# First adaLN modulation in fp32 column groups, and the sums of the later modulations moved to ScalarE and POOL

## The chip, the cores and the metric

One core of a Trainium2 chip runs the whole program. The metric is device time in microseconds, the median of several executions. Besides, one execution was recorded by the profiler.

## What is computed

A diffusion backbone of two layers works on 256 latent tokens and 256 context tokens of 1024 channels. Each layer begins with a modulation: the conditioning vector goes through SiLU and a matrix of 1024 x 6144, which gives six vectors of 1024 channels (shift, scale and gate for each of two sub-layers), for the latent and for the context stream:

```python
mod_lat = (silu_c @ w_mod[l] + b_mod[l])[:, None, :]
mod_ctx = silu_cc @ w_mod[l] + b_mod[l]
sh1, sc1, gt1, sh2, sc2, gt2 = jnp.split(mod_lat, 6, axis=-1)
h = rms_norm(x, g_pre_mix[l]) * (1.0 + sc1) + sh1
y, yc = token_mixer(h, hc, w_in[l], ...)
x = x + gt1 * rms_norm(y, g_post_mix[l])
h = rms_norm(x, g_pre_mlp[l]) * (1.0 + sc2) + sh2
x = x + gt2 * rms_norm(squared_relu_mlp(h, w_mlp_in[l], w_mlp_out[l]), g_post_mlp[l])
```

The context stream goes through the same with its own modulation; in the second layer only the latent stream is written. The token mixer has three branches (retention, neighbourhood attention, grouped-query attention) and large projections; the MLP widens to 4096. Everything is fp32.

## The kernel before

Large products are made of three fp32r matmuls: each operand is split in a rounded part (a cast on ScalarE, tiles `wh`, `pwh`) and the rest (a subtraction on VectorE, `wl`, `pwl`), and hi x hi, hi x lo and lo x hi are summed (`mm3`, line 185). Weights come in blocks of 128 x 1024 (512 KB) on SP's queue, loaded three ahead and split two ahead of the step that uses them (`ahead`, line 1411).

**The prologue** (line 243) does the first modulation (shift and scale of the first sub-layer, layer 0), the normalisation of the 512 tokens and the first product (queries and keys of the retention branch, `pr`). It goes in four quarters `kp` of 256 channels. For each, four blocks of `w_mod` and one of `w_in` are loaded. All five are split. `mod` (line 287) multiplies the conditioning vectors, stationary in `msr` (two columns of the rounded part, two of the rest, zeros up to 128), with 32 matmuls of 256 columns into `modps`; `row` (298) copies four rows out on ScalarE; `fin` (306) turns them into columns with four small matmuls (`pm`, eight records in the trace) that add the bias row; VectorE makes shift and scale; `pre_tr` transposes the normalised tokens (`ph`); `pre_h` applies scale and shift on ScalarE and splits the result on VectorE (`hT`); `gemm` (318) makes the quarter's 24 matmuls. The order of all this is written out by hand in `PLAN` (line 56): c splits up to a block, a is `mod`, t `pre_tr`, r `row`, f `fin`, h `pre_h`, g `gemm`. While `Ordered.on` is set, each engine keeps the program's order. The normalisation is a chain of small VectorE operations for each of four token tiles (`pre_xn`).

**The later modulations** (`mod_dve`, line 403) aren't on TensorE. For each of ten vectors, eight blocks `mr` of `w_mod` are loaded on POOL's queue, into two buffers; for each block and stream VectorE does one operation, acc = block x scalar + acc (`stt`, in `step`, line 459), the first one with the bias row `brow` in place of acc. Two streams: six of the vectors, one stream: four; 128 operations in all. Then the partitions are summed by TensorE: with ones (gates, `pg`) or, for shift and scale, with a stationary of 32 columns in column groups of 32 output partitions (`pmr`, line 432). The steps of three vectors are woven into the end of layer 0's mixer (line 1344), those of six more into its MLP, the last into layer 1's MLP.

The scheduler that comes with the language fixes each engine's order of instructions; `tc.issue_after(ins)` puts the instructions of a block behind `ins` in the queue of `ins`'s engine.

Of the kernel before, what the change touches and what calls it, by code (L numbers as in the profile page):

```python
# [9 lines left out]
F32 = mybir.dt.float32  # L10
# [20 lines left out]
MLB = 2  # L31
NT = 8
NB2 = 5
C1 = 0
WR = 3
WH = 3
WLD = 3
# [11 lines left out]
XLATE = True  # L49
END = ((0, 0), (1, 0))  # L50
ORD = ((0, 4, 5), (0, 4, 8))
RW = 2
PLD = 4
PAD, PAD2, WP = 432, 272, 1152
FILL = (((0, 9), (9, 21), (21, 33)), ((0, 9), (7, 22), (22, 39)))
PLAN = ["c4 t0 a0 c5 r0 f0 h0 c9 g0 c13",
        "a1 t1 r1 c14 f1 h1 c18",
        "a2 r2 c19 g1 t2 f2 h2",
        "a3 t3 r3 c20 f3 h3 g2"]


class Ordered:
# [20 lines left out]
def kernel(  # L83
# [47 lines left out]
    def S(name, dt=F32R):  # L131
        return sp.tile([128, 2, 512], dt, tag="s", name=name)
# [31 lines left out]
    def tt(o, a, b, op):  # L164
        return v_.tensor_tensor(out=o, in0=a, in1=b, op=op)
# [36 lines left out]
    selr = const.tile([4, 512], F32R, tag="selr", name="selr")  # L202
    cc = const.tile([128, 8, 2], F32, tag="cc", name="cc")
    cs = const.tile([128, 8, 2], F32, tag="cs", name="cs")
    ones = const.tile([128, 128], F32R, tag="ones", name="ones")
    oneh = const.tile([128, 32], F32, tag="oneh", name="oneh")
    onesf = const.tile([128, 128], F32, tag="onesf", name="onesf")
# [33 lines left out]


    def prologue():
        pr = []
        M = {}
        raw, rdy = {}, {}
        md = lambda kp: [wspec(w_mod[0], 512 * hf, 4, v * D + 256 * kp, 256) for v in range(2) for hf in range(2)]
        gm = lambda kp: [wspec(w_in[0], 256 * kp, 2, RQ, 512)]
        wts = md(0) + gm(0) + md(1) + gm(1) + md(2) + gm(2) + md(3) + gm(3)
        mi = (0, 5, 10, 15)  # L250
        gi = (4, 9, 14, 19)

        def load(n):
            while len(raw) < min(n, len(wts)):
                i = len(raw)
                ap, k, *_ = wts[i]
                t = S("pr", F32) if i % RW else wrp.tile([128, 2, 512], F32, tag="wr", name="pr")
                raw[i] = t
                st["hold_sp"] = nc.sync.dma_start(
                    out=t.rearrange("p a b -> p (a b)").rearrange("p (k n) -> p k n", k=k), in_=ap)  # L260

        def cut(n):
            while len(rdy) < min(n, len(wts)):
                i = len(rdy)
                load(i + PLD)
                t, k = raw[i], wts[i][1]
                hi = wtile(whp, "wh", "pwh").rearrange("p (a b) -> p a b", a=2) if i % 3 == 0 else S("pwh")
                lo = wtile(wlp, "wl", "pwl").rearrange("p (a b) -> p a b", a=2) if i % 3 == 0 else S("pwl")
                st["hold_act"] = s_.copy(hi, t)
                st["hold"] = tt(lo, t, f(hi), ALU.subtract)  # L270
                rdy[i] = [u.rearrange("p a b -> p (a b)").rearrange("p (k n) -> p k n", k=k) for u in (hi, lo)]

        def init():
            msr = S("msr")
            zero = T("zero")
            v_.memset(zero, 0.0)
            v_.tensor_copy(msr[:, 0, :], zero)
            v_.tensor_copy(msr[:, 1, :], zero)
            msr = msr.rearrange("p a b -> p (a b)").rearrange("p (k m) -> p k m", k=8)
            v_.tensor_copy(msr[:, :, 0:2], cs)  # L280
            tt(msr[:, :, 2:4], cs, f(msr[:, :, 0:2]), ALU.subtract)
            M["msr"] = msr
            for n_ in ("sh1", "sc1"):
                st[0, n_] = smp.tile([128, 8, 2], F32, tag=n_, name=n_, bufs=2)
            pr.extend(mmt(f"pr{i}") for i in range(4))

        def mod(kp):
            ps = att("modps")
            for i in range(4):
                v, hf = i // 2, i % 2  # L290
                w = rdy[mi[kp] + i]
                for k in range(4):
                    for p in range(2):
                        t_.matmul(ps[:, 256 * v:256 * v + 256], M["msr"][:, 4 * hf + k, :], w[p][:, k, :],
                                  start=(hf == 0 and k == 0 and p == 0), stop=(hf == 1 and k == 3 and p == 1))
            M["ps", kp] = ps

        def row(kp):
            s_.copy(st["r5", kp][0:4, :], M["ps", kp][0:4, :])

        def bias(kp):
            r5 = st["r5", kp] = T("r5")
            nc.gpsimd.dma_start(out=r5[4:5, :].rearrange("o (v n) -> o v n", v=2),
                                in_=b_mod[0:1, 0:2 * D].rearrange("o (v n) -> o v n", v=2)[:, :, 256 * kp:256 * kp + 256])

        def fin(kp):
            r5 = st.pop(("r5", kp))
            pt = att("pm")
            for j in range(4):
                t_.matmul(pt[:, 2 * j:2 * j + 2], r5[0:5, 128 * j:128 * j + 128], sel[0:5, 18:20],  # L310
                          start=True, stop=True)
            p3 = pt[:, 0:8].rearrange("p (j e) -> p j e", e=2)
            hs = slice(2 * kp, 2 * kp + 2)
            v_.tensor_copy(st[0, "sh1"][:, hs, :], p3[:, 0:2, :])
            for s in range(2):
                stt(st[0, "sc1"][:, hs, s], p3[:, 2:4, s], 1.0, gp[:, 0, hs], ALU.add, ALU.mult)

        def gemm(kp):
            w_ = rdy[gi[kp]]
            for k in range(2):  # L320
                for i in range(4):
                    kc = 2 * kp + k
                    w = slice(128 * i, 128 * i + 128)
                    mm3(pr[i], (w_[0][:, k, w], w_[1][:, k, w]), hpair(kc, 512), kc == 0, kc == 7)

        def go(ws):
            Ordered.on = True
            load_x(4)
            load(PLD)
            for kp in range(2):  # L330
                bias(kp)
            init()
            sq = [pre_sq(0)]
            pre_xn(0, sq[0])
            sq.append(pre_sq(1))
            cut(C1)
            pre_xn(1, sq[1])
            for kp, plan in enumerate(PLAN):
                for c in plan.replace("_", " ").split():
                    o, n = c[0], int(c[1:])  # L340
                    if o == "c":
                        cut(n)
                    elif o == "a":
                        mod(n)
                    elif o == "r":
                        row(n)
                    elif o == "t":
                        ph = [pre_tr(n, s) for s in range(2)]
                    elif o == "f":
                        fin(n)  # L350
                        if n < 2:
                            bias(n + 2)
                    elif o == "h":
                        h32 = [T("h32") for _ in range(2)]
                        for j in range(2):
                            for s in range(2):
                                pre_h(0, 0, n, s, ph[s], (j,), h32[s])
                    elif o == "g":
                        gemm(n)
            Ordered.on = False  # L360
            gemm(3)
            with tc.issue_after(st["hold"].ins):
                setup2()
            for i in range(4):
                st["qkdone"](i, pr[i])

        return [([], go)]
# [35 lines left out]
    def mod_dve(l, vec, streams):  # L403
# [52 lines left out]
                    g = gp[:, 2 * l + vec // 3, :].rearrange("p (h j) -> p h j", h=2)  # L456
                    stt(os, ps, 1.0, g, ALU.add, ALU.mult)

        def step(kc):
            def go(ws):  # L460
                w = mrp.tile([128, 2, 512], F32, tag="mr", name="mr")
# [6 lines left out]
                for s in streams:  # L468
                    if kc == 0:
                        st["acc", s] = S("acc", F32)  # L470
                    a = st["acc", s]
                    stt(a, w, cs[:, kc, s:s + 1], M["b"] if kc == 0 else a, ALU.mult, ALU.add)
            return go

        fins = [fin1, fin2] if gate else [fin2, fin3]
# [257 lines left out]
    def attn_units(l, n, kind):  # L733
# [22 lines left out]
        def s1(hs, qb):  # L756
# [51 lines left out]
            def go():  # L808
                if na and qb == 0:
                    for h in hs:  # L810
                        bt = st["bt", h] = btp.tile([128, 384], F32, tag="bt", name="bt")
                        nc.gpsimd.dma_start(out=bt, in_=relb[l, h])
                context() if qb == 2 else latent()

            return go
# [706 lines left out]
```

## Time and profile before

| | us |
|---|---|
| median of 3 runs (1461.59 to 1465.43) | 1465.25 |
| profiled execution, its own time | 1462.51 |
| its span, first to last instruction | 1460.7 |
| busy: PE, VectorE (DVE), ScalarE (ACT), POOL | 1414.4, 1070.0, 733.1, 77.6 |
| end of the prologue's last product | 71.08 |

The trace has one row for each instruction or group. A line number L74 is that of a helper that all compute instructions pass through, so that the names of the tiles tell what an instruction is: `pr` the first product, `modps` the first modulation, `mr` and `acc` a block and a sum of the later ones. "x8" is the number of instructions put together. PE is TensorE's matmul side, PEld its weight loads.

### The profile page before, as it was taken

To read this page: it belongs to the slowest core of one execution; us is meant where nothing else is said; L and a number is where in the kernel's file an instruction comes from. 1 tells how busy PE (TensorE), PEld (TensorE's weight loads), DVE (VectorE), ACT (ScalarE), POOL (GpSimd) and SP (SyncE) were. 2 spreads that over 40 slices of the span, in tenths; PEclk is the share of its full clock that TensorE was granted. 3 is DMA by queue.
4 is the path that set the end of the run, shared out by engine and by line. 5 is a ranking of instruction groups with operands and counts; after the bars stand their busy time and mean duration, and the time that the engine had idled before them with its cause. 6 is when DMAs were issued, how large, how long until landed. Compare 5 with 4: busy or idle time off the path is not lost.

```text
span 1460.7 us, 21002 instructions
## 1 busy us (share of the span) xinstructions
PE 1414.4 (97%) x7966; PEld 1209.2 (83%) x7966; DVE 1070.0 (73%) x2001; ACT 733.1 (50%) x1243; POOL 77.6 (5%) x141
## 2 busy tenths in 40 slices
PE   5999999999999999999999998899999999999997
PEld 3878888877888788988888876788889999899886
DVE  7785797787995879877755637986877886767544
ACT  5563565555423357524234154654656664577542
POOL 2000000000110000101001101000000000000000
PEclk9999999999999999999999999999999999999999
DMA  9522122222565666756546727433233446479753
GB/s 313 176 73 72 44 73 61 81 83 80 166 209 149 184 230 170 221 150 209 167 136 217 215 87 244 145 108 109 73 87 102 146 133 183 121 199 268 216 189 124
DMA packets 231957, 219.64 MB, mean 150 GB/s; under 512 B 7652, under 2 KB 188956, under 8 KB 231856
## 3 DMA queue, kind: packets, MB, share of 16 engines
q1 hardware_dynamic: 217856, 170.42, 38.2%
q0 software_dynamic: 14000, 47.88, 10.8%
q8 instruction: 62, 1.02, 0.3%
q14 instruction: 39, 0.32, 0.1%
HBM read 217.22 MB, written 1.05 MB: 149 GB/s over the span
## 4 chain that ended last, share of the span: by engine, by line
PE 83%; DVE 6%; issue 4%; DMA 4%; ACT 2%; SPq 0%; POOL 0%; DVEq 0%; ACTq 0%; POOLq 0%
PE ps L74 37%; PE pO L74 17%; PE br L74 7%; PE pB L74 6%; PE po L74 3%; PE pt L74 2%; PE sl L74 2%; DVE wl L74 2%; PE pr L74 2%; PE gkv L74 2%; DMA wr<-in_w_m_dram 1%; DMA pr<-in_w_mod_dram 1%; DVE hT L74 1%; PE ro L74 1%; PE modps L74 1%
## 5 line engine op out<-in xcount | busy, mean ns | idle before, releaser
L74 PE MATMUL ps<-hT,wh 128*128 128x256 f32 (+1 forms) x2480 | 600.8, 334 | 4.4 <-ACT wh L74 3.0
L74 ACT CAST wh<-wr 128x1024 fp32r<-128x1024 f32 x295 | 310.2, 1053 | 452.5 <-PE ps L74 170.0
L74 DVE TENSOR_TENSOR wl<-wr,wh 128x1024 fp32r<-128x1024 f32 x295 | 359.3, 1221 | 200.5 <-ACT wh L74 196.6
L74 PEld LDWEIGHTS ps<-hT,wh 128*128 128x128 f32 x2480 | 418.1, 190 | 59.2 <-ACT wh L74 7.6
L74 PE MATMUL ps<-hT,wl 128*128 128x256 f32 (+1 forms) x1240 | 411.5, 332 | 1.4 <-DVE wl L74 1.2
L74 PEld LDWEIGHTS ps<-hT,wl 128*128 128x128 f32 x1240 | 235.0, 190 | 25.2 <-DVE wl L74 2.9
L74 PE MATMUL pO<-wh,u 128*128 128x512 f32 x768 | 238.5, 390 | 0.0
L74 PEld LDWEIGHTS pO<-wh,u 128*128 128x128 f32 x768 | 144.0, 188 | 30.6 <-issue 0.8
L74 DVE SCALAR_TENSOR_TENSOR acc<-mr,cs,acc 128x1024 f32<-128x1024 f32 x112 | 140.6, 1279 | 30.5 <-DMA mr<-in_w_mod_dram 30.2
L74 PE MATMUL pO<-wl,u 128*128 128x512 f32 x384 | 149.9, 390 | 3.1 <-DVE wl L74 3.1
L74 PEld LDWEIGHTS pO<-wl,u 128*128 128x128 f32 x384 | 72.1, 188 | 19.2 <-DVE wl L74 4.2
L74 PE MATMUL pB<-wh,hT 128*128 128x512 f32 x256 | 82.3, 392 | 0.0
L462 POOL DMA_DIRECT2D mr<-in_w_mod_dram x80 | 42.7, 534 | 514.5 <-DVE acc L74 486.5
L74 PE MATMUL pO<-wh,yT 128*128 128x512 f32 x192 | 59.7, 390 | 0.0
L74 PEld LDWEIGHTS pB<-wh,hT 128*128 128x128 f32 x256 | 48.1, 188 | 9.7
L74 DVE TENSOR_TENSOR PT<-pt,PT 128x512 fp32r<-128x512 f32 x80 | 51.4, 681 | 2.4 <-ACT PT L74 1.9
L74 PE MATMUL pB<-wl,hT 128*128 128x512 f32 x128 | 49.9, 390 | 0.0
L74 ACT CAST PT<-pt 128x512 fp32r<-128x512 f32 x80 | 43.3, 599 | 8.9 <-PE pt L74 5.1
L74 DVE TENSOR_TENSOR u<-rl,u 128x256 fp32r<-128x256 f32 (+1 forms) x71 | 36.6, 516 | 9.7 <-ACT u L74 9.7
L74 PE MATMUL pt<-ident,P 128*128 128x128 f32 x320 | 41.6, 273 | 0.6 <-DVE P L74 0.6
L74 PEld LDWEIGHTS pO<-wh,yT 128*128 128x128 f32 x192 | 35.9, 188 | 7.3
L74 DVE TENSOR_SCALAR P<-P,su 128x512 f32<-128x512 f32 (+1 forms) x96 | 40.2, 439 | 1.6
(262 smaller groups left out, 1882.9 us busy)
## 6 DMA issues: line engine op xcount, KB each, us to landing
wr<-in_w_m_dram SPq DMA_DIRECT2D x143, 512.0 KB, 4.5
wr<-in_w_in_dram SPq DMA_DIRECT2D x104, 512.0 KB, 3.7
mr<-in_w_mod_dram POOLq DMA_DIRECT2D x80, 512.0 KB, 4.5
wr<-in_w_br_dram SPq DMA_DIRECT2D x24, 512.0 KB, 3.4
wr<-in_w_out_dram SPq DMA_DIRECT2D x24, 512.0 KB, 4.0
pr<-in_w_mod_dram SPq DMA_DIRECT2D x16, 512.0 KB, 6.3
bt<-in_relb_dram POOLq DMA_DIRECT2D x16, 192.0 KB, 2.8
X<-in_x_dram SPq DMA_DIRECT2D x4, 512.0 KB, 4.9
```

The source lines that it names most:

```text
L74: ins = call(*a, **k)
L462: nc.gpsimd.dma_start(out=w, in_=w_mod[l, 128 * kc:128 * kc + 128, vec * D:vec * D + D].rearrange("p (a n) -> p a n", a=2))
```

## The change

In the prologue, the 16 blocks of `w_mod` aren't split any more. They are multiplied in fp32: the stationary operand `csz` has 32 columns (two conditioning vectors, zeros), and the four partial sums over k go to four column groups of 32 output partitions; the small matmuls of `fin` then add the four groups (`selp`), and the bias is added by VectorE, from columns that one transpose makes at the start. All twenty blocks are loaded at once. `PLAN` has a new order, with modulation, transposes and small matmuls of a quarter one quarter ahead of the products, five warm-up matmuls of 512 columns at the start (`WARM`), and nine and five matmuls of zeros with 128 columns in it (`w9`, `w5`). A copy on POOL, `late`, waits for the fifteenth block; the loads of tables and of the first `mr` blocks are put behind it.

In the later modulations the product is a ScalarE operation (in place for one stream, into a new tile `mw` for the other) and the sum an addition on POOL, and the load of a block is issued one step earlier.

```diff
-PLAN = ["c4 t0 a0 c5 r0 f0 h0 c9 g0 c13",
-        "a1 t1 r1 c14 f1 h1 c18",
-        "a2 r2 c19 g1 t2 f2 h2",
-        "a3 t3 r3 c20 f3 h3 g2"]
+PLAN = "t0 a0 c0 r0 f0 w9 d0 h0 g0 a1 t1 r1 f1 c1 d1 h1 a2 r2 t2 w5 f2 g1 c2 d2 h2 a3 r3 t3 c3 f3 d3 h3 g2"
+GATE = 14
+PAD, PAD2, WP = 424, 272, 1152
+WARM = 5
...
+        def load():
+            for i, (ap, k, *_) in enumerate(wts):
+                t = wrp.tile([128, 2, 512], F32, tag="wr", name="pr") if i % 5 == 4 and i < 15 else S("pr", F32)
                 raw[i] = t
+                st["hold_sp"] = nc.sync.dma_start(out=flat(t, k), in_=ap)
+                if i == GATE:
+
+                    st["late"] = nc.gpsimd.tensor_copy(out=late, in_=t[:, 0, 0:1])
+
+        def cast(kp):
+            hi[kp] = wtile(whp, "wh", "pwh").rearrange("p (a b) -> p a b", a=2)
+            st["hold_act"] = s_.copy(hi[kp], raw[5 * kp + 4])
+
+        def cut(kp):
+            lo = wtile(wlp, "wl", "pwl").rearrange("p (a b) -> p a b", a=2)
+            st["hold"] = tt(lo, raw[5 * kp + 4], f(hi[kp]), ALU.subtract)
...
         def init():
+            w, zero = att("warm"), T("zero")
             v_.memset(zero, 0.0)
+            for _ in range(WARM):
+                t_.matmul(w, zero[:, 0:128], zero, start=True, stop=True)
+            t = S("csz", F32)
+            v_.memset(t, 0.0)
...
+            v_.tensor_copy(M["csz"][:, :, 0:2], cs)
...
+            t_.transpose(pt[:, 0:16], M["b16"][0:16, 0:128], ident[0:16, 0:16])
+            v_.tensor_copy(M["bcol"][:, 0, :], pt[:, 0:8])
+            stt(M["bcol"][:, 1, :], pt[:, 8:16], 1.0, gp[:, 0, :], ALU.add, ALU.mult)
+
+        def run_on(n):
+            w = att("warm")
+            for _ in range(n):
+                t_.matmul(w[:, 0:128], M["zero"], M["zero"], start=True, stop=True)
...
         def mod(kp):
+            ps = M["ps", kp] = att("modps")
             for i in range(4):
                 v, hf = i // 2, i % 2
+                w = flat(raw[5 * kp + i], 4)
                 for k in range(4):
-                    for p in range(2):
-                        t_.matmul(ps[:, 256 * v:256 * v + 256], M["msr"][:, 4 * hf + k, :], w[p][:, k, :],
-                                  start=(hf == 0 and k == 0 and p == 0), stop=(hf == 1 and k == 3 and p == 1))
+                    t_.matmul(ps[32 * k:32 * k + 32, 256 * v:256 * v + 256], M["csz"][:, 4 * hf + k, :], w[:, k, :],
+                              start=(hf == 0), stop=(hf == 1))
...
+            bias()
+            load()
             init()
+            early()
             sq = [pre_sq(0)]
             pre_xn(0, sq[0])
...
-            with tc.issue_after(st["hold"].ins):
+            with tc.issue_after(st["hold"].ins), tc.issue_after(st["late"].ins):
                 setup2()
...
+        def load(kc):
+            w = M["w", kc] = mrp.tile([128, 2, 512], F32, tag="mr", name="mr")
+            with tc.issue_after(st["late"].ins):
                 nc.gpsimd.dma_start(
...
+        def step(kc):
+            def go(ws):
+                if kc == 0:
+                    load(0)
+                if kc < 7:
+                    load(kc + 1)
+                w = M.pop(("w", kc))
+                for s in reversed(streams):
                     if kc == 0:
                         st["acc", s] = S("acc", F32)
                     a = st["acc", s]
-                    stt(a, w, cs[:, kc, s:s + 1], M["b"] if kc == 0 else a, ALU.mult, ALU.add)
+
+                    m = a if kc == 0 else w if s == 0 else S("mw", F32)
+                    s_.activation(m, w, AF.Copy, scale=cs[:, kc, s:s + 1])
+                    nc.gpsimd.tensor_tensor(out=a, in0=m, in1=M["b"] if kc == 0 else a, op=ALU.add)
```

## Rows read from the trace of the kernel before

**Rows 1.** The page's part 1: busy us (share of the span) xinstructions of each engine
```profile
PE 1414.4 (97%) x7966; PEld 1209.2 (83%) x7966; DVE 1070.0 (73%) x2001; ACT 733.1 (50%) x1243; POOL 77.6 (5%) x141
```

**Rows 2.** Stretches: us, busy by engine (xinstructions), granted clock, DMA share, GB/s
```profile
0.00:20.00 20.00, 5.59 (x19) 4.02 (x20) 12.92 (x45) 8.22 (x13) 9.02 (x20) 1.00 0.91 314
20.00:30.00 10.00, 6.34 (x35) 5.20 (x34) 6.37 (x14) 6.82 (x10) 0.00 (x0) 0.89 1.07 379
30.00:40.00 10.00, 10.00 (x48) 8.56 (x47) 9.28 (x9) 6.46 (x7) 0.00 (x0) 0.77 0.77 256
...
365.00:500.00 135.00, 134.99 (x614) 110.14 (x613) 117.15 (x129) 43.37 (x61) 16.82 (x30) 1.00 0.59 177
590.00:905.00 315.00, 310.84 (x1432) 254.72 (x1432) 202.44 (x207) 119.68 (x165) 35.07 (x62) 1.00 0.60 184
```

**Rows 3.** The chain of waits, 20 to 75 us: start us, us, what
```profile
24.88 0.58 ACT r L74
...
25.51 1.06 PE pm L74 x8
...
28.47 8.60 PE pr L74 x24
37.07 3.83 PE modps L74 x32
...
42.75 4.02 PE modps L74 x32
46.77 5.47 PE pr L74 x24
...
59.97 11.11 PE pr L74 x48
```

**Rows 4.** Timeline of PE, 448 to 456 us: start us, us, what
```profile
449.76 1.07 PE L74 MATMUL pmr<-acc,oneh 128*32 128x512 f32 x8
450.75 0.73 PE L74 MATMUL ps<-hT,wh 128*128 128x512 f32 x2
```

**Rows 5.** Groups of instructions, 0 to 75 us: busy us, mean ns, idle before
```profile
L74 ACT CAST pwh<-pr 128x1024 fp32r<-128x1024 f32 x20 | 20.0, 1054 | 6.6 <-DMA pr<-in_w_mod_dram 6.4 <-DMA pr<-in_w_in_dram 0.2
...
L74 DVE TENSOR_TENSOR pwl<-pr,pwh 128x1024 fp32r<-128x1024 f32 x20 | 23.5, 1220 | 8.1 <-ACT pwh L74 8.0
```

**Rows 6.** Timeline of VectorE, 0 to 16 us: start us, us, what
```profile
3.18 0.48 DVE L74 MEMSET zero<- 128x512 f32 x1
...
6.34 0.15 DVE L74 TENSOR_SCALAR pv<-pms 128x1 f32<-128x1 f32 x1 [1.36 <-ACT xj L74]
...
15.21 0.75 DVE L74 TENSOR_SCALAR X<-X,py 128x1024 f32<-128x1024 f32 x1
```

**Rows 7.** Timeline of PE, first quarter of the first modulation
```profile
20.26 0.41 PE L74 MATMUL modps<-pwh,msr 128*128 128x256 f32 x1
20.47 0.41 PE L74 MATMUL modps<-pwl,msr 128*128 128x256 f32 x1
...
22.66 0.28 PE L74 MATMUL modps<-pwl,msr 128*128 128x256 f32 x1
22.78 0.28 PE L74 MATMUL modps<-pwh,msr 128*128 128x256 f32 x1
```

**Rows 8.** Later sums: POOL's groups from 365 to 500 us, the page's groups and DMA issues
```profile
L462 POOL DMA_DIRECT2D mr<-in_w_mod_dram x24 | 12.8, 534 | 120.6 <-DVE acc L74 120.6
L466 POOL MEMSET brow<- 128x1024 f32 x2 | 2.0, 976 | 0.0
...
L74 DVE SCALAR_TENSOR_TENSOR acc<-mr,cs,acc 128x1024 f32<-128x1024 f32 x112 | 140.6, 1279 | 30.5 <-DMA mr<-in_w_mod_dram 30.2
...
mr<-in_w_mod_dram POOLq DMA_DIRECT2D x80, 512.0 KB, 4.5
```

**Rows 9.** Waits of PE, 590 to 905 us: who for whom, us, times, longest
```profile
PE pO L74 <- DVE wl L74: 2.7, 1, 2.7
PE pmr L74 <- DVE acc L74: 1.1, 1, 1.1
```

More of the change, by code (lines that the diff above doesn't have):

```diff
@@ L33 @@
 NB2 = 5
-C1 = 0
 WR = 3
@@ L51 @@
 ORD = ((0, 4, 5), (0, 4, 8))
-RW = 2
-PLD = 4
-PAD, PAD2, WP = 432, 272, 1152
 FILL = (((0, 9), (9, 21), (21, 33)), ((0, 9), (7, 22), (22, 39)))
-PLAN = ["c4 t0 a0 c5 r0 f0 h0 c9 g0 c13",
-        "a1 t1 r1 c14 f1 h1 c18",
-        "a2 r2 c19 g1 t2 f2 h2",
-        "a3 t3 r3 c20 f3 h3 g2"]
+PLAN = "t0 a0 c0 r0 f0 w9 d0 h0 g0 a1 t1 r1 f1 c1 d1 h1 a2 r2 t2 w5 f2 g1 c2 d2 h2 a3 r3 t3 c3 f3 d3 h3 g2"
+GATE = 14
+PAD, PAD2, WP = 424, 272, 1152
+WARM = 5
 class Ordered:
@@ L204 @@
     cs = const.tile([128, 8, 2], F32, tag="cs", name="cs")
+    late = const.tile([128, 1], F32, tag="late", name="late")
     ones = const.tile([128, 128], F32R, tag="ones", name="ones")
@@ L245, in prologue @@
         M = {}
-        raw, rdy = {}, {}
+        raw, hi, rdy = {}, {}, {}
         md = lambda kp: [wspec(w_mod[0], 512 * hf, 4, v * D + 256 * kp, 256) for v in range(2) for hf in range(2)]
@@ L249, in prologue @@
         wts = md(0) + gm(0) + md(1) + gm(1) + md(2) + gm(2) + md(3) + gm(3)
[L250 to L257, printed above, removed]
-                raw[i] = t
-                st["hold_sp"] = nc.sync.dma_start(
-                    out=t.rearrange("p a b -> p (a b)").rearrange("p (k n) -> p k n", k=k), in_=ap)
@@ L262, in cut @@
[L262 to L271, printed above, removed]
+        flat = lambda t, k: t.rearrange("p a b -> p (a b)").rearrange("p (k n) -> p k n", k=k)
@@ L273, in init, with bias @@
+        def cut(kp):
+            lo = wtile(wlp, "wl", "pwl").rearrange("p (a b) -> p a b", a=2)
+            st["hold"] = tt(lo, raw[5 * kp + 4], f(hi[kp]), ALU.subtract)
+            rdy[kp] = [flat(u, 2) for u in (hi[kp], lo)]
+        def bias():
+            M["b16"] = T("b16")
+            nc.gpsimd.dma_start(out=M["b16"][0:16, 0:128], in_=b_mod[0, 0:2 * D].rearrange("(r n) -> r n", n=128))
         def init():
-            msr = S("msr")
-            zero = T("zero")
+            w, zero = att("warm"), T("zero")
@@ L276, in init @@
             v_.memset(zero, 0.0)
[L277 to L282, printed above, removed]
+            for _ in range(WARM):
+                t_.matmul(w, zero[:, 0:128], zero, start=True, stop=True)
+            t = S("csz", F32)
@@ new lines, in init @@
+            v_.memset(t, 0.0)
+            M["csz"], M["selp"] = t[:, 0, 0:256].rearrange("p (k m) -> p k m", k=8), t[:, 1, 0:2]
+            M["zero"], M["bcol"] = t[:, 1, 128:256], t[:, 1, 2:18].rearrange("p (v k) -> p v k", v=2)
+            v_.tensor_copy(M["csz"][:, :, 0:2], cs)
+            for j in range(4):
+                r = slice(32 * j, 32 * j + 2)
+                v_.tensor_copy(M["selp"][r, :], ident[r, r])
+            pt = att("bt")
+            t_.transpose(pt[:, 0:16], M["b16"][0:16, 0:128], ident[0:16, 0:16])
@@ L283, in init, with early @@
+            v_.tensor_copy(M["bcol"][:, 0, :], pt[:, 0:8])
[4 more added lines that the diff above has]
+                t_.matmul(w[:, 0:128], M["zero"], M["zero"], start=True, stop=True)
+        def early():
             for n_ in ("sh1", "sc1"):
@@ L287, in mod @@
         def mod(kp):
-            ps = att("modps")
+            ps = M["ps", kp] = att("modps")
             for i in range(4):
                 v, hf = i // 2, i % 2
-                w = rdy[mi[kp] + i]
+                w = flat(raw[5 * kp + i], 4)
                 for k in range(4):
-                    for p in range(2):
-                        t_.matmul(ps[:, 256 * v:256 * v + 256], M["msr"][:, 4 * hf + k, :], w[p][:, k, :],
-                                  start=(hf == 0 and k == 0 and p == 0), stop=(hf == 1 and k == 3 and p == 1))
-            M["ps", kp] = ps
+                    t_.matmul(ps[32 * k:32 * k + 32, 256 * v:256 * v + 256], M["csz"][:, 4 * hf + k, :], w[:, k, :],
+                              start=(hf == 0), stop=(hf == 1))
         def row(kp):
[L299 to L304, printed above, removed]
+            r = M["r", kp] = T("r5")
+            s_.copy(r, M["ps", kp])
         def fin(kp):
-            r5 = st.pop(("r5", kp))
+            r = M.pop(("r", kp))
             pt = att("pm")
             for j in range(4):
-                t_.matmul(pt[:, 2 * j:2 * j + 2], r5[0:5, 128 * j:128 * j + 128], sel[0:5, 18:20],
-                          start=True, stop=True)
+                t_.matmul(pt[:, 2 * j:2 * j + 2], r[:, 128 * j:128 * j + 128], M["selp"], start=True, stop=True)
             p3 = pt[:, 0:8].rearrange("p (j e) -> p j e", e=2)
             hs = slice(2 * kp, 2 * kp + 2)
-            v_.tensor_copy(st[0, "sh1"][:, hs, :], p3[:, 0:2, :])
             for s in range(2):
-                stt(st[0, "sc1"][:, hs, s], p3[:, 2:4, s], 1.0, gp[:, 0, hs], ALU.add, ALU.mult)
+                tt(st[0, "sh1"][:, hs, s], p3[:, 0:2, s], M["bcol"][:, 0, hs], ALU.add)
+            for s in range(2):
+                tt(st[0, "sc1"][:, hs, s], p3[:, 2:4, s], gp[:, 0, hs], ALU.mult)
+            for s in range(2):
+                tt(st[0, "sc1"][:, hs, s], st[0, "sc1"][:, hs, s], M["bcol"][:, 1, hs], ALU.add)
         def gemm(kp):
-            w_ = rdy[gi[kp]]
+            w_ = rdy[kp]
             for k in range(2):
@@ L328, in go @@
             load_x(4)
-            load(PLD)
-            for kp in range(2):
-                bias(kp)
+            bias()
+            load()
             init()
+            early()
             sq = [pre_sq(0)]
@@ L335, in go @@
             sq.append(pre_sq(1))
-            cut(C1)
             pre_xn(1, sq[1])
[L338 to L359, printed above, removed]
+            ph = {}
+            for c in PLAN.split():
+                o, n = c[0], int(c[1:])
+                if o == "c":
+                    cast(n)
+                elif o == "d":
+                    cut(n)
+                elif o == "a":
+                    mod(n)
+                elif o == "r":
+                    row(n)
+                elif o == "w":
+                    run_on(n)
+                elif o == "t":
+                    ph[n] = [pre_tr(n, s) for s in range(2)]
+                elif o == "f":
+                    fin(n)
+                elif o == "h":
+                    h32 = [T("h32") for _ in range(2)]
+                    for j in range(2):
+                        for s in range(2):
+                            pre_h(0, 0, n, s, ph[n][s], (j,), h32[s])
+                elif o == "g":
+                    gemm(n)
             Ordered.on = False
             gemm(3)
-            with tc.issue_after(st["hold"].ins):
+            with tc.issue_after(st["hold"].ins), tc.issue_after(st["late"].ins):
                 setup2()
@@ L457, in fin3 @@
                     stt(os, ps, 1.0, g, ALU.add, ALU.mult)
-        def step(kc):
-            def go(ws):
-                w = mrp.tile([128, 2, 512], F32, tag="mr", name="mr")
+        def load(kc):
+            w = M["w", kc] = mrp.tile([128, 2, 512], F32, tag="mr", name="mr")
+            with tc.issue_after(st["late"].ins):
                 nc.gpsimd.dma_start(
@@ L467, in go @@
                     nc.gpsimd.dma_start(out=M["b"][0:1], in_=b_mod[l:l + 1, vec * D:vec * D + D].rearrange("o (a n) -> o a n", a=2))
-                for s in streams:
+        def step(kc):
[6 more added lines that the diff above has]
+                for s in reversed(streams):
                     if kc == 0:
@@ L811, in go @@
                         bt = st["bt", h] = btp.tile([128, 384], F32, tag="bt", name="bt")
-                        nc.gpsimd.dma_start(out=bt, in_=relb[l, h])
+                        with tc.issue_after(st["late"].ins):
+                            nc.gpsimd.dma_start(out=bt, in_=relb[l, h])
                 context() if qb == 2 else latent()
```

## The prediction

> **What bounds the kernel now.** I read the page's first part, then stretches, then the chain of waits, then single engines. The page shows TensorE busy for 97% of the span [rows 1], so time can go only where PE is idle or does work that the change takes away. The stretches show where that is [rows 2]: PE is busy for 5.59 of the first 20 us and 6.34 of the next 10, then without a gap; in the two stretches that hold the sums of the later modulations it is busy for 134.99 of 135 us (365 to 500) and 310.84 of 315 us (590 to 905). The granted clock reads 0.77 from 30 to 40 us. So the first modulation can give much, the later ones at most the 4.2 us of idle PE.
>
> The chain [rows 3] says what ends the prologue: from 28.47 us on every piece is PE: first product, second quarter's modulation, transposes, third quarter's modulation and so on, until the last two products end at 71.08. Before 28.47 it goes through the copy of the modulation sums, the small transposing matmuls, VectorE and ScalarE. The first product took 8.60 us for its 24 matmuls, the second 5.47: the same work at the low and at the high clock.
>
> **The change, part by part.** I sum against the profiled execution (1462.51 us, span 1460.7; 2.7 us under the median of 1465.25) and apply the difference to the median, as the changed kernel will also be given as one.
>
> *Modulation products.* A quarter's 32 fp32r matmuls of 256 columns took 3.83 us in the second quarter and 4.02 in the third [rows 3]; the fourth took as long as the third. They become 16 fp32 matmuls in four column groups. The nearest row: four fp32 products of 512 columns in four such groups, eight records, start at 449.76 and the next work at 450.75 [rows 4], 0.99 us a set. A quarter is four sets of half the columns: 4 x 0.50 = 2.0 us; if a set cost the same at half its columns it would be 3.96 and nothing would be gained. I take 2.0, since the time of long matmuls goes with columns. Quarters two to four: 11.87 - 6.0 = 5.9 us less on the chain. Of the 20 casts and 20 subtractions, 16 each go (1.05 and 1.22 us each [rows 5]); from 28.47 on the chain holds none of them, so that is worth nothing there.
>
> *Clock.* If it is up when the first product begins: 8.60 - 5.47 = 3.1 less. The five run-on matmuls ahead of the third quarter's small transposes are 128 columns of fp32, a quarter of a set: 5 x 0.25 = 1.2 more, on PE's path. So from first product to the end of the prologue: now 71.08 - 28.47 = 42.6, then 42.6 - 5.9 - 3.1 + 1.2 = 34.8 us.
>
> *Up to the first product* there is a new wait. Everything is kept in program order: five warm-up matmuls (fp32, 512 columns), the transpose of the bias, VectorE's two operations on it, and only then VectorE's normalisation. VectorE now zeroes the tile at 3.18 (0.48 us), starts normalising at 6.34 and ends at 15.96 [rows 6], a chain of 9.62 us. The warm-up begins at 3.66 and costs 5 x 0.99 = 5.0 us at the high clock, 9.9 at the low. At 20.26 and 20.47 the 256-column matmuls are 0.21 apart, at 22.66 and 22.78 0.12 [rows 7]: PE starts low and rises only after it has been at work since 16 us. I take the middle, 7.4: warm-up ends at 11.1, bias done about 12.0, normalised at 21.6, last transposes 22.1 (0.5 us now), modulation at the low clock 2 x 2.0 to 26.1, copy and its hand-overs 0.6 (0.58 [rows 3]) to 26.7, small matmuls 1.06 to 27.8. From their end to the first product it is 1.90 us now (26.57 to 28.47); VectorE gets a 1.22 us subtraction and three small operations (0.3) ahead of the operand, and 0.6 of ScalarE hides under these: 2.8, so 30.6. Nine run-on matmuls lie beside this: 2.2 us at the high clock, 4.5 at the low. In all 2.1 us later than now; prologue ends at 30.6 + 34.8 = 65.4, **5.7 us earlier**.
>
> *Loads.* All twenty are issued at once on SP's queue. X and the first quarter are 8 x 0.524 = 4.2 MB; at 314 GB/s (first 20 us [rows 2]) there by about 14 us plus the start, before 22. X and all twenty blocks are 12.6 MB, with the two tables and two blocks that POOL sends once the fifteenth block is in, 14.0: 45 us. The fourth modulation is reached after the first product (30.6 + 5.5), the second quarter's modulation with both transposes (3.9), the third's (2.9), run-on (1.2), small matmuls (1.0) and the second product (5.5), at 50.6. Hidden. What waits behind the gate on POOL (the tables for rope and decay) needs some 6 issues of 0.53 after about 32 us and is first read after the prologue, the bias tables far later. Zero, and without that cover as much as they land late.
>
> *Later sums.* VectorE loses 128 operations of 1.28 us [rows 8], 164 us; ScalarE gains 128 of 1.05 (same shape as its casts), 134 us; POOL gains 128 additions of a price T that no row shows. Bounds: POOL writes 1024 columns in 0.976 us [rows 8]; two reads in turn give 1.95, two reads and a write in turn 2.93. VectorE's 1.22 for this shape is a floor from further off. I take 2.2, nearer the end where writes overlap reads, as they do on VectorE. The tightest stretch, 365 to 500, has 48 additions, 24 loads of 0.534 (12.8 us), two clearings (2.0) and four small loads (2.1): 105.6 + 12.8 + 4.1 = 122.5 of 135 us. ScalarE there: 43.4 [rows 2] + 48 x 1.05 = 93.8. The new waits: ScalarE's product waits for its block, whose buffer POOL's addition must have freed; behind it in ScalarE's queue stand the weight casts, for which VectorE's subtraction and PE wait. Two blocks take 0.53 + 4.5 (landing [rows 8]) + 1.05 + 2T = 10.5 us, 5.2 a block, against 135/24 = 5.6. The second stretch has 72 additions in 315 us and more room. So no loss, and of PE's waits there (2.7 for a subtraction, 1.1 for a sum [rows 9]) I count 2 us as gone; the wait for the sum stays, as the sum now ends on a slower engine.
>
> Of the addition the Trainium skill, GPSIMD Engine Reference, section Elementwise, states 4497 ns for 2048 fp32 columns; half is 2.25 as an estimate, and the sum would stay as it is. No run here shows it yet.
>
> Sum: -5.7 - 2 = -7.7; 1454.8 against the profiled execution, **1457 us** against the median.
>
> **Rivals.** *POOL is too slow.* With T = 2.93 the first stretch needs 140.6 + 16.9 = 157.5 of 135 us: 22.5 over. ScalarE then waits for blocks, the casts behind it come late, and PE with them: 1465.25 - 5.7 + 22.5 = **1482**, slower. It decides at T = (135 - 16.9)/48 = 2.46. For it: VectorE's two-input work in that stretch goes on beside POOL, and no row shows the two together; PE's slack is nil by [rows 2]. Against: two tiles of weights are cut ahead, which lends some us. The Trainium skill speaks for this rival: SBUF — State Buffer, section Who interferes with whom, says that a VectorE instruction with two SBUF inputs and a GpSimd instruction that reads SBUF exclude each other while one runs. By that rule T would be longer in effect and the subtractions late as well. Nothing in this trace shows it, as POOL never reads there.
>
> *Normalisation isn't held*, because the warm-up is over early. Then the first modulation begins near 16.5 as now, the first product at 25.0, the prologue ends at 59.8, 11.3 earlier: with the 2 us **1452**. For: it needs only a cheaper fp32 matmul than [rows 4] implies. Against: program order and 5 x 0.99 us.
>
> *The first part gains nothing*: the clock stays low through warm-up (2.5 more), run-on (1.7 more) and first product (3.1 more), 7.3 of the 7.7 gone: **1465**. For: the low clock that the first product has now, [rows 2]. Against: nine fillers stand in the gap where it fell.
>
> **How the numbers follow.** Forecast 0.44 (own range 1450 to 1461), the second rival 0.20, the third 0.13, POOL too slow 0.23. About 0.3% (4.4 us) is what a measurement can tell here. Faster by more: 0.44 + 0.20 = 0.64; within: 0.13; slower: 0.23. The range reaches from a held clock with a short warm-up, 1446, to most of the POOL case, 1480; some 0.07 lies under it and 0.10 over.
>
> **What would show it.** The profile after: prologue's last product ending near 65 instead of 71; modulation quarters of 2.0 us of PE from the second on; first product near 30 us at 5.5 us; VectorE's first normalising operation near 12; additions on POOL at 2.2 us start to start and PE still above 134 of 135 us while they run. Wrong would be: long PE waits for weights on ScalarE between 350 and 500 (POOL too slow), or a first product before 27 us.

## The result, and the profile after

The changed kernel takes 1587.99 us (median of 4 runs, 1583.9 to 1591.44) against 1463.42 (4 runs) for the kernel before: ratio 1.0849, 95% interval 1.0821 to 1.0876. It is slower by 125 us where 1457 us was forecast and the range ended at 1480. The profiled execution took 1591.44 us, its span is 1589.7. Medians and ratios, here and below, are of runs in the fast state; the one slow run, 2754.82 us with the additions back on VectorE, is left out.

The page's part 1 and, of part 2, PE, POOL and the granted clock in 40 slices:

```profile
PE 1456.9 (92%) x8005; PEld 1229.0 (77%) x8005; DVE 1067.7 (67%) x1873; ACT 851.6 (54%) x1355; POOL 400.6 (25%) x267
...
PE   6999999999679599899887889899999999999997
...
POOL 1000000006695700476693460500000000006000
PEclk8999999999898799999998999999999999999999
```

Against [rows 1] three things stand out. PE's idle time (span less busy) went from 46.3 to 132.8 us. Its busy time rose by 42.5 with almost the same matmuls; the granted clock is lower where POOL is busy. And VectorE, which lost 128 operations of 1.28 us, is as busy as before: 1067.7 against 1070.0. Some 160 us of work went away and came back as something else.

Stretches (busy us of PE, its weight loads, VectorE, ScalarE, POOL, each with its instructions; then granted clock, DMA share, GB/s):

```profile
365.00:500.00 135.00, 109.23 (x464) 87.41 (x465) 78.29 (x63) 64.41 (x72) 90.24 (x54) 0.89 0.42 129
...
590.00:905.00 315.00, 275.93 (x1318) 229.05 (x1317) 212.14 (x229) 181.41 (x247) 167.15 (x102) 0.93 0.49 152
```

From 365 to 500 PE had 134.99 busy us [rows 2], now 109.23. The prologue is another matter. The chain of waits, 20 to 75 us (start, length, what):

```profile
28.89 5.94 PE pr L70 x24
34.83 1.86 PE modps L70 x32
...
41.39 1.12 PE warm L70 x10
...
43.30 5.59 PE pr L70 x24
```

Beside [rows 3]: a quarter's modulation is 1.86 us instead of about 4, the first product 5.94 instead of 8.60, and the matmuls that follow the prologue's last product (`pB`) start at 63.41 instead of 70.92. So the prologue gained 7.5 us and the later sums lost some 130. VectorE and POOL around 400 us (start, length, engine, line, operation, result<-operands, shapes):

```profile
394.24 2.10 DVE L70 TENSOR_TENSOR wl<-wr,wh 128x1024 fp32r<-128x1024 f32 x1 [1.25 <-ACT wh L70]
396.26 0.68 DVE L70 SCALAR_TENSOR_TENSOR tg<-tg,br 128x512 f32<-128x512 f32 x1
...
399.78 5.02 DVE L70 TENSOR_TENSOR yacc<-yacc,tg 128x512 f32<-128x512 f32 x1
404.80 6.08 DVE L70 TENSOR_TENSOR wl<-wr,wh 128x1024 fp32r<-128x1024 f32 x1
```

```profile
395.22 3.38 POOL L496 TENSOR_TENSOR acc<-mr,acc 128x1024 f32<-128x1024 f32 x1
...
399.49 2.40 POOL L496 TENSOR_TENSOR acc<-mw,acc 128x1024 f32<-128x1024 f32 x1
401.85 2.40 POOL L496 TENSOR_TENSOR acc<-mr,acc 128x1024 f32<-128x1024 f32 x1
404.54 0.57 POOL L475 DMA_DIRECT2D mr<-in_w_mod_dram  x1 [0.30 <-POOL acc L496]
405.13 2.36 POOL L496 TENSOR_TENSOR acc<-mw,acc 128x1024 f32<-128x1024 f32 x1
407.44 2.35 POOL L496 TENSOR_TENSOR acc<-mr,acc 128x1024 f32<-128x1024 f32 x1
410.08 0.57 POOL L475 DMA_DIRECT2D mr<-in_w_mod_dram  x1 [0.30 <-POOL acc L496]
```

Here the cause shows; the experiments below test it. The `yacc` addition, 0.69 us where nothing disturbs it (the prologue-only kernel below), starts at 399.78 beside POOL's first addition and ends at 404.80: POOL's two additions end at 404.25, and it ends 0.55 us later, near its own 0.69. The weight subtraction after it (1.22 us in [rows 5]) ends at 410.88, POOL's next two additions at 409.79. Each of these two waits through two POOL additions and gets in while POOL issues a transfer. The `tg` operation at 396.26, whose `br` lies in PSUM (TensorE's result memory) and not in SBUF (the on-chip memory of the tiles), takes 0.68 us beside a running addition. Groups of VectorE, 365 to 500 us (count | busy us, mean ns | idle before and what ended it):

```profile
L70 DVE TENSOR_TENSOR wl<-wr,wh 128x1024 fp32r<-128x1024 f32 x17 | 37.4, 2204 | 33.3 <-ACT wh L70 33.3
L70 DVE TENSOR_TENSOR yacc<-yacc,tg 128x512 f32<-128x512 f32 x10 | 19.1, 1906 | 0.3
```

And groups of the page's part 5, over the span:

```profile
L496 POOL TENSOR_TENSOR acc<-mr,acc 128x1024 f32<-128x1024 f32 x70 | 183.5, 2621 | 26.3 <-ACT mr L70 25.7
...
L496 POOL TENSOR_TENSOR acc<-mw,acc 128x1024 f32<-128x1024 f32 x42 | 102.2, 2432 | 55.2 <-ACT mw L70 54.5
L70 ACT ACTIVATE mr<-mr,cs 128x1024 f32<-128x1024 f32 x70 | 80.2, 1149 | 61.1 <-DMA mr<-in_w_mod_dram 54.4
```

The additions take 2.35 to 2.40 us undisturbed, 2.4 to 2.6 in the mean of the groups and 3.4 at worst. Of PE's longest waits in the whole run (us in total, times, longest):

```profile
PE pmr L70 <- POOL acc L496: 31.7, 4, 12.4
...
PE ps L70 <- DVE wl L70: 13.3, 6, 6.0
PE pg L70 <- ACT ahi L70: 12.0, 1, 12.0
```

The finished sums come late (`pmr`, `pg`), and so do weights and operands from VectorE.

### The profile page after: what moved, and what is told of

Read it like the earlier page. It is cut to its first block, busy times and chain, and to the rows that moved or that the text cites. A ratio compares the mean times of both kernels' runs of the same rounds, so it can differ in the third digit from the quotient of the medians.

```text
span 1589.7 us, 21192 instructions
## 1 busy us (share of the span) xinstructions
PE 1456.9 (92%) x8005; PEld 1229.0 (77%) x8005; DVE 1067.7 (67%) x1873; ACT 851.6 (54%) x1355; POOL 400.6 (25%) x267
## 3 DMA queue, kind: packets, MB, share of 16 engines
HBM read 217.22 MB, written 1.05 MB: 137 GB/s over the span
## 4 chain that ended last, share of the span: by engine, by line
issue 37%; PE 32%; POOL 15%; DVE 6%; DMA 5%; ACT 4%; SPq 1%; DVEq 0%; POOLq 0%; ACTq 0%
PE ps L70 13%; POOL acc L496 13%; PE pO L70 6%; DMA mr<-in_w_mod_dram 3%; DVE wl L70 3%; PE pB L70 3%; PE br L70 2%; PE pt L70 1%; PE po L70 1%; PE pr L70 1%; POOL mr L475 1%; ACT wh L70 1%; SPq L256 1%; PE sl L70 1%; ACT mw L70 1%
## 5 line engine op out<-in xcount | busy, mean ns | idle before, releaser
L70 DVE TENSOR_TENSOR wl<-wr,wh 128x1024 fp32r<-128x1024 f32 x295 | 467.5, 1587 | 322.5 <-ACT wh L70 318.7
L70 PE MATMUL ps<-hT,wh 128*128 128x256 f32 (+1 forms) x2480 | 619.6, 342 | 23.9 <-DVE z L70 18.1
L70 PEld LDWEIGHTS ps<-hT,wh 128*128 128x128 f32 x2480 | 430.7, 195 | 83.4 <-issue 29.2
L70 PE MATMUL ps<-hT,wl 128*128 128x256 f32 (+1 forms) x1240 | 420.9, 340 | 13.5 <-DVE wl L70 13.3
L496 POOL TENSOR_TENSOR acc<-mr,acc 128x1024 f32<-128x1024 f32 x70 | 183.5, 2621 | 26.3 <-ACT mr L70 25.7
L837 POOL DMA_DIRECT2D bt<-in_relb_dram x16 | 8.6, 539 | 571.5 <-DVE m L70 571.5
L496 POOL TENSOR_TENSOR acc<-mw,acc 128x1024 f32<-128x1024 f32 x42 | 102.2, 2432 | 55.2 <-ACT mw L70 54.5
L70 ACT ACTIVATE mr<-mr,cs 128x1024 f32<-128x1024 f32 x70 | 80.2, 1149 | 61.1 <-DMA mr<-in_w_mod_dram 54.4
L70 ACT ACTIVATE mw<-mr,cs 128x1024 f32<-128x1024 f32 x42 | 47.9, 1149 | 79.5 <-DMA mr<-in_w_mod_dram 79.1
L70 DVE TENSOR_TENSOR u<-rl,u 128x256 fp32r<-128x256 f32 (+1 forms) x71 | 73.6, 1038 | 19.6 <-ACT u L70 19.3
```

The lines of the kernel that those rows point to most:

```text
L70: ins = call(*a, **k)
L496: nc.gpsimd.tensor_tensor(out=a, in0=m, in1=M["b"] if kc == 0 else a, op=ALU.add)
```

## The experiments

Theory C, from the traces above: POOL's additions and VectorE's operations with two operands in SBUF keep each other out. Rivals: S, POOL's additions are simply too long for the time there is; B, the loads wait for buffers that POOL frees; A, ScalarE's products hold the casts queued behind them. Expectations are quoted as written before each run.

**The two parts apart.** The prologue alone (the sums on VectorE, loaded as before, the loads behind `late`), and the sums alone in the old prologue:

```diff
-                    stt(a, w, cs[:, kc, s:s + 1], M["b"] if kc == 0 else a, ALU.mult, ALU.add)
+                    m = a if kc == 0 else w if s == 0 else S("mw", F32)
+                    s_.activation(m, w, AF.Copy, scale=cs[:, kc, s:s + 1])
+                    nc.gpsimd.tensor_tensor(out=a, in0=m, in1=M["b"] if kc == 0 else a, op=ALU.add)
```

> The changed prologue with the later sums as before, on VectorE. The theory that the whole loss lies in the later sums: as the first product ended at 63.41 in place of 71.08 us, some 7.7 us faster than before, ratio 0.992 to 0.997, and PE busy for over 134 of 135 us in the stretch of the sums. The rival, that the changed prologue delays what follows it (tables behind the gate): no faster than before, or slower.

> The old prologue with the later sums on ScalarE and POOL. If the two parts add up: 124 + 8 = 132 us slower than before, near 1595. If the early prologue made the sums worse (other order of instructions): clearly less, under 1560.

Prologue alone: 1458.26 us, ratio 0.9947 [0.9924, 0.9971]. Sums alone (the diff above put into the kernel before, with the early load): 1596.77, ratio 1.0898 [1.0861, 1.0935]. The parts add up: -8 and +131 us of 1464 make the change's +124. In the prologue-only kernel PE's 8005 matmuls, as many as in the changed one, are busy for 1419.2 of 1458.3 us; so of the 131.4 us between the two spans 93.7 are idle PE and 37.7 the same matmuls at a lower clock (0.952 in the mean against 0.988). As expected, PE is busy for 134.99 of 135 us in the stretch of the sums when the prologue alone is changed; this stretch and two groups of VectorE in it are what the next runs are set against:

```profile
365.00:500.00 135.00, 134.99 (x612) 109.26 (x611) 116.38 (x125) 42.06 (x56) 16.45 (x30) 1.00 0.61 183
```

```profile
L70 DVE TENSOR_TENSOR wl<-wr,wh 128x1024 fp32r<-128x1024 f32 x24 | 28.9, 1216 | 6.6 <-ACT wh L70 6.5
L70 DVE TENSOR_TENSOR yacc<-yacc,tg 128x512 f32<-128x512 f32 x14 | 9.5, 685 | 0.2
```

**Additions back on VectorE, and free buffers**, each in the changed kernel:

```diff
-                    nc.gpsimd.tensor_tensor(out=a, in0=m, in1=M["b"] if kc == 0 else a, op=ALU.add)
+                    nc.vector.tensor_tensor(out=a, in0=m, in1=M["b"] if kc == 0 else a, op=ALU.add)
```

```diff
-                    m = a if kc == 0 else w if s == 0 else S("mw", F32)
+                    m = a if kc == 0 else S("mw", F32)
```

> As changed, but the additions on VectorE; ScalarE's products, their waits for blocks and the early loads stay. Theory P (POOL's additions are the cause, by their own length or by holding VectorE up): back to within 10 us of the prologue alone, 1450 to 1465. Theory A (ScalarE's queue held by products that wait for blocks): at least 40 us of the loss stays, over 1500.

> As changed, but both streams' products go into tiles of their own, so that a block's buffer is free when ScalarE has read it and no load waits for POOL. Theory B (the loads, and with them ScalarE's queue, hang on POOL's additions through the block buffers): over half of the loss goes, under 1525. Theories P (POOL too slow or in VectorE's way): less than 25 us goes, over 1560.

With ScalarE's products kept and the addition on VectorE: 1466.07 (7 runs), ratio 1.001 [0.9986, 1.0034], 8 us over the prologue alone (9 by the ratios): that is the most that ScalarE's part costs (A). With both products out of place, so that no load waits for POOL: 1574.15, ratio 1.0743 [1.0702, 1.0785]. B explains some 15 us of the loss; under the other theories less than 25 were expected to go.

**Work on POOL that nobody waits for**, in the prologue-only kernel: after each block's load five or three (two streams or one) additions that read SBUF, or twelve or seven clearings that only write it, over the same 424 columns:

```diff
+                with tc.issue_after(ld.ins):
+                    r = rel.rearrange("p a b -> p (a b)")[:, 0:PAD]
+                    for _ in range(5 if len(streams) == 2 else 3):
+                        nc.gpsimd.tensor_tensor(out=padt, in0=r, in1=r, op=ALU.add)
```

```diff
+                with tc.issue_after(ld.ins):
+                    for _ in range(12 if len(streams) == 2 else 7):
+                        nc.gpsimd.memset(padt, 0.0)
```

> The prologue alone (sums on VectorE), and beside it additions on POOL that nobody waits for: 5 of 424 columns a block (3 where there is one stream), about 5 us of POOL time, behind the block's load. Theory C (a POOL addition and a VectorE operation with two SBUF inputs keep each other out): VectorE's subtractions of 128x1024, 1.22 us without them, take over 1.6 us on average from 365 to 500 us, and the kernel is over 20 us slower than the prologue alone. Theory S (the sum on POOL is only slow, and PE waits for its end): subtractions stay at 1.22, and the time within 10 us, for loads that wait behind the additions.

> The same with clears in place of the idle additions, which write 424 columns and read nothing, 12 a block (7), again about 5 us of POOL time. Both theories: subtractions stay near 1.22 us and the kernel within 10 us of the prologue alone. Against theory C would be the same stretching as with additions.

Idle additions: 1582.42, ratio 1.0814 [1.0751, 1.0878]. Idle clearings: 1473.99, ratio 1.005 [0.9991, 1.0109]. The additions' profile, 365 to 500 us (stretch, then groups of VectorE), and POOL's group over the span:

```profile
365.00:500.00 135.00, 110.71 (x447) 87.32 (x446) 107.56 (x90) 30.91 (x45) 120.52 (x100) 0.87 0.43 129
```

```profile
L70 DVE SCALAR_TENSOR_TENSOR acc<-mr,cs,acc 128x1024 f32<-128x1024 f32 x28 | 46.2, 1681 | 16.9 <-DMA mr<-in_w_mod_dram 16.9
L70 DVE TENSOR_TENSOR wl<-wr,wh 128x1024 fp32r<-128x1024 f32 x16 | 28.5, 1793 | 0.2 <-ACT wh L70 0.2
L70 DVE TENSOR_TENSOR yacc<-yacc,tg 128x512 f32<-128x512 f32 x9 | 9.6, 1072 | 0.1
...
L485 POOL TENSOR_TENSOR pad<-rel 128x424 f32<-128x424 f32 x336 | 447.6, 1332 | 25.3 <-DMA rel<-in_rel_dram 3.7
```

and the clearings', same views:

```profile
365.00:500.00 135.00, 131.39 (x580) 106.74 (x579) 111.69 (x119) 39.47 (x52) 104.38 (x224) 0.97 0.58 176
```

```profile
L70 DVE TENSOR_TENSOR wl<-wr,wh 128x1024 fp32r<-128x1024 f32 x21 | 25.3, 1218 | 7.1 <-ACT wh L70 7.0
...
L484 POOL MEMSET pad<- 128x424 f32 x800 | 365.4, 457 | 40.5
```

This is the pair that decides. Nobody reads the results of either; POOL is busy for 120.52 and 104.38 of the 135 us. Beside reading additions VectorE's subtraction takes 1.79 us and the addition 1.07, PE loses 24 us in the stretch and the kernel nearly all that the change lost. With the additions PE waits for VectorE's weights above all: its three largest waits for `wl` are 75.5 us together. Beside writes the subtraction stays at 1.22 and the kernel loses about 15 us on the prologue alone (1.005 against 0.9947). That is more than the 10 us that both theories allowed; the interval of 1.005 reaches some 9 us either way, and no run shows where they go. Not quite alike: in both kernels VectorE still has the 128 sums, which idle additions hold too (1.68 instead of 1.28).

**The additions' reads taken out**, in the changed kernel: three clearings of the same tiles in place of each addition, all dependencies kept. The ten later modulations come out as zeros.

```diff
-                    nc.gpsimd.tensor_tensor(out=a, in0=m, in1=M["b"] if kc == 0 else a, op=ALU.add)
+                    nc.gpsimd.memset(m, 0.0)
+                    nc.gpsimd.memset(a, 0.0)
+                    nc.gpsimd.memset(a[:, 0, :], 0.0)
```

> The changed kernel with each addition on POOL replaced by three clears (the product's tile, the sum, half of the sum again: 2560 columns, 2.4 us): who waits for whom and POOL's time stay, only POOL reads nothing. The later modulations come out as zeros. Theory S: most of the loss stays, over 1550. Theory C: over half of it goes, under 1525, and the subtractions are back at 1.22 us.

1461.01 us, ratio 0.9977 [0.995, 1.0005]. The stretch, groups of VectorE in it, and of POOL over the span:

```profile
365.00:500.00 135.00, 131.35 (x585) 107.28 (x586) 63.28 (x76) 86.03 (x94) 107.48 (x149) 0.97 0.54 170
```

```profile
L70 DVE TENSOR_TENSOR wl<-wr,wh 128x1024 fp32r<-128x1024 f32 x22 | 26.9, 1223 | 43.7 <-ACT wh L70 43.7
...
L497 POOL MEMSET acc<- 128x1024 f32 x128 | 122.4, 965 | 1.0
L498 POOL MEMSET acc<- 128x512 f32 x128 | 67.3, 532 | 1.1
L496 POOL MEMSET mr<- 128x1024 f32 x70 | 67.1, 959 | 87.0 <-ACT mr L70 86.8
```

POOL works 0.96 + 0.97 + 0.53 = 2.46 us for each sum, a little more than an addition alone, in the same order and with the same waits, and the loss is gone but for some 4 us against the prologue alone (0.9977 and 0.9947, with intervals that overlap). So neither POOL's length (S) nor the waits on it cost much: that the additions read does. Of operations that read only additions were tried.

**Half of it**: the context stream's sums on VectorE, the latent's as changed.

```diff
+                    if s == 1:
+                        stt(a, w, cs[:, kc, s:s + 1], M["b"] if kc == 0 else a, ALU.mult, ALU.add)
+                        continue
```

> The changed kernel with the context stream's sums on VectorE as before, only the latent stream's on ScalarE and POOL: 2.4 + 0.57 us of POOL a block, less than the 4.2 us at which the blocks came before. Theory S: the loss goes, within 10 us of the prologue alone. Theory C: POOL still holds VectorE up for half the time, and a third to a half of the loss stays, 1495 to 1530.

1531.43 us, ratio 1.0466 [1.04, 1.0531]. Set against the prologue alone (0.9947 of 1462.08, 1454) that is 77 us for 80 additions, as the full change is 131 for 128: about 1.0 us of the kernel for each. It is 59% of the loss and just over the 1530 expected, as 80 of the 128 sums (63%), and not half, stay on POOL.

**The prologue's own limits.** The prologue-only kernel again; with VectorE's two operations on the bias behind the normalisation; and this with one warm-up matmul in place of five:

```diff
             pt = att("bt")
             t_.transpose(pt[:, 0:16], M["b16"][0:16, 0:128], ident[0:16, 0:16])
+            M["pt"] = pt
+
+        def bcol():
+            pt = M["pt"]
             v_.tensor_copy(M["bcol"][:, 0, :], pt[:, 0:8])
...
             pre_xn(1, sq[1])
+            bcol()
```

```diff
-WARM = 5
+WARM = 1
```

> The prologue alone once more, on the same chip as the next two kernels, so that these can be set against it. Every theory: as in its first run, ratio 0.993 to 0.997, the normalisation's first operation near 10.4 us, the first product near 28.9.

> The two operations on the bias stand behind the normalisation in VectorE's queue. Theory that they hold the normalisation: it starts near 6.3 us in place of 10.4, and the first product some 4 us earlier, at 25; the time is 3 to 4 us under the prologue alone, near 1454, ratio 0.992. Rival, something else holds the first product just as long (the loads of the first quarter of w_mod, or the clock): the normalisation starts early all the same, but the first product moves by less than 1.5 us and the time by less than 1.5.

> As the kernel before it, with one warm-up matmul of 512 columns in place of five. If the warm-up raises the clock for the first modulation and the first product: both get slower, the first modulation toward 4 us, the first product toward 8.6 in place of 5.9, and the time is 2 to 4 us above the one with five. If the clock at the first product comes from the run-on matmuls just ahead of it: the first product still takes 5.5 to 6 us and the time is the same within 1 us.

In this order: 1456.9 us, ratio 0.9958 [0.9936, 0.9979]; 1455.2, ratio 0.9944 [0.9919, 0.9968]; 1450.09, ratio 0.991 [0.9882, 0.9937]. With the bias moved the normalisation starts at 5.82 instead of 11.15 us, but the first product moves only from 29.71 to 26.60, and the time fell by 1.7 us, inside the intervals: between the two theories. (In this repeat the warm-up took 7.10 us, 0.7 more than the first time, and what follows is as much later.) The third shows why, and neither of its expectations came: the time is 5 us lower, not higher and not the same. PE from 5 to 27.5 us (stretch, busy PE, granted clock, DMA share, GB/s), with five and with one:

```profile
5.00:10.00 5.00, 5.00 (x9) 1.00 1.02 365
10.00:15.00 5.00, 1.61 (x7) 0.98 1.08 390
15.00:20.00 5.00, 4.47 (x35) 0.50 1.08 386
20.00:27.50 7.50, 6.82 (x29) 0.50 1.08 390
```

```profile
5.00:10.00 5.00, 1.44 (x3) 1.00 1.01 357
10.00:15.00 5.00, 1.38 (x4) 1.00 1.09 392
15.00:20.00 5.00, 4.28 (x35) 1.00 1.08 385
20.00:27.50 7.50, 6.52 (x40) 1.00 1.08 388
```

After five warm-up matmuls and a stretch with little work the granted clock is at its lower level, 1.2 GHz, from 15 to 27.5 us; with one it reads 2.4 GHz throughout. With five the small matmuls take 1.86 us and the run-on ahead of the first product 4.19, with one 1.05 and 2.25, and PE goes from the run-on into the first product without a gap: PE itself held it. With one the first product starts at 24.15, the prologue's last matmul at 58.52 instead of 61.42. This kernel is the fastest of all, 0.991 of the one before; its interval overlaps that of the kernel with five a little.

## Why the prediction was wrong

**What failed** is the step on the later sums, "So no loss", put at -2 us where the sums alone measured +131. It priced an addition on POOL by its own length and asked whether POOL and ScalarE have room. The length was nearly right: 2.2 us taken, 2.40 measured undisturbed, under the 2.46 at which the sum of the stretch tipped (2.53 in the mean of all 128, VectorE's hold on POOL included); ScalarE's product was 1.15 us for 1.05. The room was there, too: with clearings of 2.46 us in place of the additions some 4 us are lost. What the step left at nothing is what a reading POOL does to VectorE. The subtractions went from 1.22 to 2.20 us and `yacc` from 0.69 to 1.91 in the tight stretch, each held one waiting out the addition that runs and sometimes a second; the 164 us that VectorE was to be spared came back as waiting inside its instructions, POOL was held as well, weights and sums came late, PE fell idle for 94 us more, and the same matmuls took 38 us longer at a lower granted clock.

**The rival "POOL is too slow"** had the right sign, and the sentence beside it the right mechanism: by the Trainium skill, SBUF — State Buffer, section Who interferes with whom, a VectorE instruction with two SBUF inputs and a GpSimd instruction that reads SBUF exclude each other, and one that only writes does not. The idle additions against the idle clearings agree: 1.79 against 1.22 us for the subtraction. But the rival's price was worked out from POOL's length again, 22.5 us in one stretch. Taking turns put into the same sum would hardly have raised it: VectorE's subtractions and `yacc` additions in that stretch of the trace before are 36 us, and with POOL's 122.5 that makes 159 of 135 us, 24 over (an estimate). In the traces the third vector's sum on PE (`pmr`) starts at 556.0 us with the change and at 496.6 with the prologue alone, the ninth's at 1023.3 and 898.0: 59 us lost by then, 66 more from there on, where the rival counted none. So the size seems to lie in how late weights and sums reach PE, not in an engine that is full (POOL is busy for 90.24 of the 135 us); no run separates what each of them costs. I also counted "VectorE's two-input work goes on beside POOL" as evidence for the rival, yet gave it only 0.23, because no row before shows the two engines reading together. A resource that the trace has never shown in shared use calls for a wide price, not a small chance.

**Point by point.** Modulation quarter: 2.0 us forecast, 1.86. Run-on ahead of the third quarter's small matmuls: 1.2, 1.12. First product: 5.5, 5.94 (the 8.60 before ran at the lower clock for its first half only, as its matmuls come 0.43 us apart up to 34 us and then 0.23), and its start 30.6, 28.89: the warm-up took 6.28 us instead of 7.4, so the normalisation, held by the bias as forecast (near 12), began at 10.41. Prologue: 5.7 us earlier forecast, 7.5 in the trace, 6 to 8 in the two timed comparisons of the prologue alone. Loads hidden: PE's list of waits names none in the prologue. "Normalisation isn't held" did not come about in the changed kernel; made true by two edits it gave 1450, near the 1452 it was priced at, with the first product at 24.15 (25.0) and the prologue over at 58.9 (59.8); that the times agree so well is in part luck, as the 1452 counts 2 us from the later sums, which are on VectorE there. "The first part gains nothing" fell. A block's cycle on POOL was forecast at 5.2 us, against 5.6 available; in the trace above the loads are issued 5.5 to 5.6 us apart while POOL runs undisturbed, so POOL keeps pace there and VectorE pays for it. The sign named for "POOL too slow", long PE waits for ScalarE's weights, did not come (4.5 us in all for `wh`); PE waited for VectorE's and for the sums.

## What to carry over

Before moving an elementwise sum to POOL, list what VectorE does with two SBUF operands in the same stretch, and its casts and scalings from SBUF to SBUF: such operations and POOL's additions take turns, and here an addition of 2.4 us cost the kernel 1.0 us although POOL had room. Price the move by the engine that is kept out, and test it by giving POOL the same work with no one waiting: one run shows the price. A warm-up that is followed by idle time should be tried shorter.

## What the runs showed that was not expected

POOL and VectorE do not always alternate one for one. Most of the held subtractions and `yacc` additions in the changed kernel waited out one POOL addition: the one at 394.24 above got in between two, and POOL's second took 3.38 us. Others saw POOL's next addition go ahead and got through when POOL turned to issuing a transfer (5.02 and 6.08 us above). What decides this is not shown. With short idle additions the subtraction waited less, 1.79 us in the mean.

Operations with one tensor operand in SBUF can be held too. Between the idle additions VectorE's casts `hT<-h` (128x256) took 0.98 to 0.99 us (40 to 47 us) instead of 0.29. And in the kernel where POOL only clears, two scalings in place (`P`, the attention weights) took 6.80 us together (361.57 to 368.37 us), while POOL cleared from 361.24 to 368.21 with one transfer to issue between; the next two, right after, took 0.62. PE waited 6.1 us for `P` in that run. So clearings leave the subtractions alone, but not every VectorE operation.

With five warm-up matmuls the granted clock fell some us after them. In each of the ten kernels with five the granted clock from 15 to 20 us is 0.50 to 0.64, in the three others (the kernel before, the sums alone, one warm-up) 1.00. Left open: the first quarter's modulation takes 3.4 to 3.6 us in either case, against 1.86 for the later quarters, though with one warm-up the granted clock reads 1.00 there.
